# Way down of a seven-product FFN: five groups of four blocks and a tail of two, instead of four groups, a small one and a tail of four

## The chip, the cores and the metric

The kernel runs on one core of a Trainium2 chip. It is one launch, and the metric is the device time of that launch in microseconds (us), taken from several runs of the same program. TensorE (PE in the profile, with PEld for its weight loads) multiplies, VectorE (DVE), ScalarE (ACT) and GpSimd (POOL) work on tiles, SyncE (SP) issues most DMAs and ScalarE some.

## The reference, cut to what matters

One layer of a hybrid decoder on 1024 prompt rows and 32 sample rows, width 1024, hidden width 2816. Four mixers stand between two FFNs; the change touches the FFNs and the norms behind them.

```python
def swiglu(x, wg, wu, wd):
    return (jax.nn.silu(x @ wg) * (x @ wu)) @ wd

def trunk_layer(x, p, gla_h0, rwkv_s0, shift0, pasts):
    ng = p['norms']
    h = x + 0.5 * rms_norm(swiglu(rms_norm(x, ng[0]), p['ff_gate'][0], p['ff_up'][0], p['ff_down'][0]), ng[1])
    cols = rms_norm(h, ng[2]) @ p['w_in']
    ...
    mix = jnp.concatenate([o_gla, o_gmlp, o_rwkv, o_dil], axis=-1) @ p['w_out']
    h = h + rms_norm(mix, ng[3])
    h = h + 0.5 * rms_norm(swiglu(rms_norm(h, ng[4]), p['ff_gate'][1], p['ff_up'][1], p['ff_down'][1]), ng[5])
```

## The kernel before

**Operands.** Everything is float32. Each matrix operand is kept as two parts, hi and lo, in the type that TensorE multiplies fast (`fp32r`); a product is three matmuls, hi·hi, hi·lo and lo·hi. So each operand has to be *split* before use: ACT copies x into hi, and POOL or DVE subtracts, lo = x - hi. Where DVE subtracts, `lower` lets ACT copy x into a PSUM bank first (`via`, tag "pt", two banks).

**Stages of an FFN.** The 2816 hidden columns are 22 blocks of 128. (1) The head makes the first two blocks with ordinary products (`gu`, `act`). (2) `body` makes the other 20 in ten pairs, each pair with one `seven` for gate and one for up, so 20 calls of `seven` per FFN. (3) `way_down` multiplies the blocks, read back from DRAM, with the third weight. (4) `tail` adds the last blocks by ordinary products, row tile after row tile, and runs the norm and the residual (`follow`, `inverse`) on each tile as it becomes ready. In the trace the first FFN's body runs to about 505 us, its way down to 721, its tail to 778, followed by the opening products of the mixers, which wait for the tiles that `follow` has normalised. In the second FFN the body runs from 1833 to 2276, the way down to 2492, and the tail to the end at 2554.

**`seven`** (L549-608) computes four blocks of a product by Winograd's scheme of seven block products; since the prompt rows are taken in three thirds of 352 columns, it has eleven products of 12 matmuls each (`prod`, L540-547). Weights A11, A12, A21, A22 are blocks as they are, S1 to S4 are sums of them. Its operands t1 to t4 are sums of the inputs; `sums` builds them once per FFN, in V (DVE) and G (POOL) operations with splits by `lower`. Results gather in PSUM: Y (tag "pg"), V ("pu"), Z ("pd"), C1 and C2 (both "pt"), two banks a tag. Y gathers S2, S3 and A22 on top of A11; after A11, S2 and S3 an ACT copy (L578) takes the partial sum out before the next product goes on top of it. Order of the products: Y A11, C1 A11, C1 A12, Z A12, C2 A21, Y S2, V S1, Y S3, C2 A22, Y A22, V S4. Only A11, A12, A21 with C1, Z, C2, and A22 with C2, use inputs without sums. `blocks` makes the eight weights in pairs in the order (A11, A12), (A21, S2), (S1, S3), (A22, S4), each in one of four rotating buffers.

**`way_down`** (L778-825) goes through groups of hidden blocks by another seven-product scheme: `GROUPS` has four groups of 4 blocks and one of 2, `NR` = 18, four "rest" blocks for the tail. Each group has four steps (`NS` = 20), a step for a pair of token tiles. A step has seven products of 6 matmuls of 512 columns (3 in the last, small group), all at L712 (`product`). Around each product hang small jobs: `hidden(s + 1)`, in seven parts, forms and splits the next step's hidden operands (POOL sums, ACT copies, DVE subtractions through `via`); `fetch(s + 2)` issues three DMAs that read hidden blocks; `jobs` hands out the next group's weight loads (`raws`), weight forms (`form`, seven per group) and the products of the 32 sample rows (`sample`, L685, 32-column strips). `late` and `split_rest` prepare the tail's operands during the last two groups. What the first group needs is begun by hooks in the last `seven` of the body (`begin_down`, `first_forms`). `Places` and `FORMS` say where each of these lies in SBUF.

**Order.** The engines do not simply follow the file: a list scheduler fixes the order on each engine beforehand, by simulated times and dependencies. In the tails (a loom of generators, `keep(KA)` and `keep(KE)`) DVE and POOL keep the order in which instructions were given.

**Tail norms.** `gain_rows` loads a gain row; for the norms behind the FFNs POOL halves it (L238). `follow` multiplies a tile by the gain on POOL (L287), `inverse` gets the inverse root on DVE from nine or so 128x1 operations (L263 to L273), and L292 multiplies by it and adds the residual.

Of the kernel before, what the change touches and what calls it, by code (L numbers as in the profile page):

```python
# [50 lines left out]
class Layer:  # L51
# [176 lines left out]
    def gain_rows(self, g, half):  # L228

        nc, src = self.nc, self.I["norm_gains"][0]  # L230
        self.junk = self.xs.tile([128, D], mybir.dt.bfloat16, name="junk", tag="s2")
        self.gr = [self.sp.tile([128, n], F32, name="gr", tag=t, bufs=b) for n, t, b in ((D, "n3", 1), (256, "ta", 2))]
        self.dma(self.gr[0], src[g:g + 1].to_broadcast([128, D]))
        for j in range(4):
            self.dma(self.gr[1][32 * j:32 * j + 32], src[g:g + 1, 256 * j:256 * j + 256].to_broadcast([32, 256]))
        if half:
            for x in self.gr:
                nc.gpsimd.tensor_scalar(x, x, 0.5, None, op0=OP.mult)  # L238

    def inverse(self, parts, i):  # L240

# [27 lines left out]
        for _ in range(3):  # L269
# [3 lines left out]
            nc.vector.scalar_tensor_tensor(y, t, 1.5, y, op0=OP.add, op1=OP.mult)  # L273
        yield
        return y

    def follow(self, y, i, name, res, out, hn=None, nxt=None):
# [10 lines left out]

        r = yield from self.inverse([(v[:, cs], (name, i, j), gained(cs)) for j, cs in enumerate(halves)], i)
        rv = res.view(i)  # L290
# [56 lines left out]

GROUPS = [(4 * i, 4) for i in range(4)] + [(16, 2)]
NR = 18
NS = 4 * len(GROUPS)  # L350


class Ffn:
# [86 lines left out]
    def sums(self):  # L440
# [13 lines left out]
        for k in range(KH):  # L454
# [14 lines left out]
            for i, (x, (hi, lo)) in enumerate(((t1, s1[k]), (t2, self.xt[0][k]), (t3, self.xt[1][k]), (t4, self.xt[2][k]))):  # L469
                nc.scalar.copy(hi, x)  # L470
                self.lower(lo, x, hi)
                if i == 1:
                    yield
            yield

    def via(self, x):


        n = x.shape[1:]
        p = self.L.ps.tile([128, 512], F32, name="via", tag="pt", bufs=2)[:, :int(np.prod(n))]  # L480
        if len(n) == 3:
# [3 lines left out]

    def lower(self, lo, x, hi):
        self.L.nc.vector.tensor_tensor(lo, self.via(x), hi.bitcast(F32), op=OP.subtract)  # L487

# [60 lines left out]
    def seven(self, c, j, sil, hooks={}):  # L549
# [26 lines left out]
        def copy(i, p):  # L576
            v = self.temp(i)
            nc.scalar.copy(v, p)  # L578
            return v

        self.prod(Y, A11, self.b11, True)
# [95 lines left out]
    def sample(self, g, which):  # L677
# [3 lines left out]
        strips = [i for i in which if i in (0, 3)], [i for i in which if i in (1, 2)]  # L681
        for j in range(4):
            at = [(i, u) for i in strips[j // 2] for u in range(n)]
            for i, u in at:
                nc.tensor.matmul(p[32 * j:32 * j + 32, :256], self.h8[:, i // 2 * n + u], self.B[i][:, u, j % 2 * 256:j % 2 * 256 + 256],  # L685
                                 start=(i, u) == at[0], stop=(i, u) == at[-1], skip_group_check=True)
        m = 128 if strips[1] else 64
# [3 lines left out]
    def form(self, g, i):  # L691
# [12 lines left out]
        for f in range(n):  # L704
            nc.gpsimd.tensor_tensor(lo[:, f], v[:, f], hi[:, f].bitcast(F32), op=OP.subtract)  # L705
        self.forms[g, i] = hi, lo
# [24 lines left out]
    def split_rest(self, i):  # L731
# [5 lines left out]
        nc.gpsimd.tensor_tensor(lo, x, hi.bitcast(F32), op=OP.subtract)  # L737
        if i < 3:
            self.fetch_rest(i + 1)

    def jobs(self, g, p):
# [3 lines left out]

        last = g + 2 == len(GROUPS)
        if g + 1 == len(GROUPS):
            return self.late(p)
        if p == 0:
            out = [(1, lambda: self.form(0, 4)), (2, lambda: self.sample(0, (3,))), (4, lambda: self.form(0, 6))] if g == 0 else [(1, lambda: self.form(g, 6))]  # L750
            return out + [(5, lambda: self.raws(g + 1, range(4 if last else 3)))]
        if p == 1:
            return [(0, lambda: self.sample(g + 1, range(4 if last else 3)))] + forms((1, 0), (3, 1)) + [(4, lambda: self.fetch_rest(0))] * last
        if p == 2:
            return forms((1, 2), (3, 3)) + [(4, (lambda: self.split_rest(0)) if last else lambda: self.raws(g + 1, (3,)))]
        return [(1, lambda: None if last else self.sample(g + 1, (3,))), *forms((1, 4), (3, 5))] + [(5, lambda: self.split_rest(1))] * last

# [7 lines left out]
    def late(self, p):  # L765

        L = self.L

        def ends():
            self.ends(self.hg[-1], 4)  # L770
# [71 lines left out]

FORMS = ((0, 1, 2, 3, 4, 5, 6), (7, 8, 9, 10, 11, 0, 1), (4, 5, 2, 3, 6, 7, 8), (9, 10, 11, 0, 1, 4, 5))


class Places:
# [28 lines left out]
    def raw(self, g, i, room, n):  # L875
        if g + 1 == len(GROUPS):
            return self.rw[i // 2][:, i % 2 * 512:i % 2 * 512 + 512]
        return (self.r0 if g == 0 else room.rearrange("p a b -> p (a b)"))[:, :1024] if i == 0 else self.rw[min(i - 1, 1)]

    def form(self, g, i):  # L880
        if g + 1 == len(GROUPS):
            v = self.x[2 + i // 2][i % 2] if i < 6 else self.x[5][0]
            return v[:, :512], v[:, 512:1024]
        u = FORMS[g][i]
# [6 lines left out]
    def rest(self, i):  # L891
        return [self.ya[:, k * T:k * T + TP] for k in (2 * (i ^ 2), 2 * (i ^ 2) + 1)]

# [2236 lines left out]
```

## Time and profile before

| | |
|---|---|
| median of 3 runs | 2565.74 us (2552.23 to 2567.77) |
| the profiled execution | 2555.89 us |
| its span in the trace | 2554.2 us |
| mean granted TensorE clock over the span | 0.971 |
| matmuls / VectorE / ScalarE / GpSimd instructions | 15519 / 3249 / 2285 / 948 |

The profile shows one execution: for each engine its busy time and, in the list of waits, what ended its idle time. A row of a timeline is start and duration in us, engine, source line, operation, output <- inputs, shape, and in brackets the idle time ahead of it with what released it. A row of the table by stage is the window, its length, then busy us (and instructions) of PE, PEld, DVE, ACT and POOL, the granted clock as a share of full speed, the share of DMA time and GB/s. A group row has busy us and mean ns of one, then the idle time ahead. Neighbouring matmuls overlap, so a single row shows a latency that is longer than the distance between starts; prices are taken from distances.

### The profile page before, as it was taken

The page shows a single profiled execution, that of the slowest core. Times are in us where ns is not written, and L with a number is a line of the kernel's source. Part 1 is how long each engine was busy: PE and PEld are TensorE (multiplying, and loading weights), DVE is VectorE, ACT ScalarE, POOL GpSimd, SP SyncE. Part 2 cuts the span into 40 slices and gives each one's busy share as a digit, 9 for nine tenths or more (in the row PEclk, how much of TensorE's full clock was granted, in tenths as well). Part 3 has the DMA queues.
Part 4 walks back from the last instruction along what each step waited for, and adds up shares of the span by engine and source line. Part 5 has one row for each costly group of instructions (what it writes and reads, how often), then busy time and mean ns, then how long its engine had stood idle before and what let it go on. Part 6 is the DMA issues. An engine that isn't in the chain of part 4 may idle for free. (4 is left out here: it accounts for less than half of the span.)

```text
span 2554.2 us, 41284 instructions
## 1 busy us (share of the span) xinstructions
PE 2447.9 (96%) x15519; PEld 2226.6 (87%) x15519; DVE 1417.8 (56%) x3249; ACT 1050.2 (41%) x2285; POOL 1093.1 (43%) x948
## 2 busy tenths in 40 slices
PE   8999999999989999999999999998999999999988
PEld 7999999967789988888888888867899999987767
DVE  7545454457776046765532567338834444446767
ACT  5433333466545243233225434335533333356642
POOL 3655555577543232242111111115255555557653
PEclk9999999999999999999989899998999999999998
DMA  4222222333333332331226667254122222233323
GB/s 130 76 72 84 68 84 70 99 103 92 109 125 120 103 105 76 90 103 50 73 68 199 188 189 229 81 185 138 66 63 82 67 83 67 84 103 100 105 88 137
DMA packets 277582, 265.23 MB, mean 104 GB/s; under 512 B 36667, under 2 KB 251860, under 8 KB 277382
## 3 DMA queue, kind: packets, MB, share of 16 engines
q1 hardware_dynamic: 227778, 212.69, 28.2%
q10 hardware_dynamic: 49604, 49.90, 5.7%
q8 instruction: 122, 2.00, 0.3%
q14 instruction: 78, 0.64, 0.1%
HBM read 195.26 MB, written 67.16 MB: 103 GB/s over the span
## 5 line engine op out<-in xcount | busy, mean ns | idle before, releaser
L516 POOL TENSOR_TENSOR wlo<-wraw,whi 128x512 fp32r<-128x512 f32 x280 | 379.4, 1373 | 329.6 <-ACT whi L515 328.9
L545 PE MATMUL p<-xh,whi 128*128 128x352 f32 x1120 | 364.1, 325 | 4.5 <-DVE hid L487 4.5
L547 PE MATMUL p<-xh,wlo 128*128 128x352 f32 x1120 | 362.6, 324 | 0.0
L546 PE MATMUL p<-xl,whi 128*128 128x352 f32 x1120 | 361.6, 323 | 0.0
L515 ACT CAST whi<-wraw 128x512 fp32r<-128x512 f32 x280 | 166.4, 620 | 407.2 <-PE p L546 293.3
L139 PE MATMUL pw<-xh,whi 128*128 128x352 f32 x888 | 309.5, 349 | 2.8 <-ACT stg L2733 2.3
L112 POOL TENSOR_TENSOR wlo<-wraw,whi 128x1024 fp32r<-128x1024 f32 x61 | 145.8, 2392 | 369.3 <-ACT whi L111 327.5
L142 PE MATMUL pw<-xl,whi 128*128 128x352 f32 x888 | 296.4, 334 | 0.0
L143 PE MATMUL pw<-xh,wlo 128*128 128x352 f32 x888 | 294.9, 332 | 0.0
L545 PEld LDWEIGHTS p<-xh,whi 128*128 128x128 f32 x1120 | 211.7, 189 | 4.8 <-DVE hid L487 4.8
L546 PEld LDWEIGHTS p<-xl,whi 128*128 128x128 f32 x1120 | 211.9, 189 | 0.0
L547 PEld LDWEIGHTS p<-xh,wlo 128*128 128x128 f32 x1120 | 210.9, 188 | 0.0
L139 PEld LDWEIGHTS pw<-xh,whi 128*128 128x128 f32 x888 | 172.2, 194 | 12.2 <-issue 6.0
L142 PEld LDWEIGHTS pw<-xl,whi 128*128 128x128 f32 x888 | 172.8, 195 | 2.8 <-issue 1.9
L143 PEld LDWEIGHTS pw<-xh,wlo 128*128 128x128 f32 x888 | 172.3, 194 | 1.9 <-issue 1.2
L545 PE MATMUL p<-hid,whi 128*128 128x352 f32 x400 | 130.0, 325 | 1.2 <-ACT n L578 1.2
L547 PE MATMUL p<-hid,wlo 128*128 128x352 f32 x400 | 130.0, 325 | 0.0
L546 PE MATMUL p<-hid,whi 128*128 128x352 f32 x400 | 129.5, 324 | 0.0
L712 PE MATMUL p<-xh,hid 128*128 128x512 f32 x336 | 113.8, 402 | 5.2 <-DVE hid L788 2.8
L788 DVE TENSOR_TENSOR y<-y,p 128x512 f32<-128x512 f32 x124 | 83.5, 683 | 36.8 <-PE p L712 33.6
L111 ACT CAST whi<-wraw 128x1024 fp32r<-128x1024 f32 x61 | 64.0, 1049 | 92.9 <-PE pw L142 53.2
L788 DVE TENSOR_TENSOR hid<-hid,p 128x512 f32<-128x512 f32 x124 | 83.7, 683 | 32.0 <-PE p L712 28.1
(657 smaller groups left out, 6014.2 us busy)
## 6 DMA issues: line engine op xcount, KB each, us to landing
wraw<-in_w_ff_gate_dram SPq DMA_DIRECT2D x44, 512.0 KB, 3.7
wraw<-in_w_ff_up_dram SPq DMA_DIRECT2D x44, 512.0 KB, 4.0
wraw<-in_w_in_dram SPq DMA_DIRECT2D x37, 512.0 KB, 5.2
wraw<-in_w_ff_down_dram SPq DMA_DIRECT2D x32, 512.0 KB, 3.6
hid_d<-tmp ACTq DMA_DIRECT2D x60, 176.0 KB, 1.9
hid_d<-n ACTq DMA_DIRECT2D x60, 176.0 KB, 2.1
whi<-hid_d SPq DMA_DIRECT2D x72, 128.0 KB, 3.5
cv<-in_cache_win_dram SPq DMA_DIRECT2D x36, 256.0 KB, 3.2
```

The costliest lines, as they stand in the source:

```text
L111: nc.scalar.copy(hi, raw)
L112: nc.gpsimd.tensor_tensor(lo, raw, hi.bitcast(F32), op=OP.subtract)
L139: ins = nc.tensor.matmul(out, a, xh[:, cs], start=(first and i == 0), stop=False)
L142: nc.tensor.matmul(out, a, xl[:, cs], start=False, stop=False)
L143: nc.tensor.matmul(out, b, xh[:, cs], start=False, stop=(last and i == n - 1))
L515: nc.scalar.copy(t[0][:, i], v)
L516: nc.gpsimd.tensor_tensor(t[1][:, i], v, t[0][:, i].bitcast(F32), op=OP.subtract)
L545: nc.tensor.matmul(out, ah, xh, start=first and k == 0, stop=False, skip_group_check=True)
L546: nc.tensor.matmul(out, ah, xl, start=False, stop=False, skip_group_check=True)
L547: nc.tensor.matmul(out, al, xh, start=False, stop=k == KH - 1, skip_group_check=True)
L712: nc.tensor.matmul(out, a[i][:, u], b[j][:, u], start=first and u == i == j == 0, stop=u == n - 1 and i == 1, skip_group_check=True)
L788: (nc.vector.tensor_copy if i % 2 else nc.scalar.copy)(v, p) if copy else nc.vector.tensor_add(v, v, p)
```

## The change

- `GROUPS` becomes five groups of four, `NR` = 20, two rest blocks. `NS` stays 20; the special cases of the small group go from `jobs`, `Places.raw` and `Places.form`; `FORMS` has five rows; `late` fetches, loads and splits the rest during the last group.
- `seven`: the products without sums, C1 and C2, come first, then Z, V S1, and S2, S3 and A22 of Y with their copies, then V S4. The hooks move.
- `sums` puts its `via` copies into "pd" instead of "pt".
- The last `seven` starts group 0 of the way down sooner: `sample` and forms 0 and 1 at hook 5, `fetch(0)` and form 2 at hook 8, the hidden operands and form 3 at hook 9.
- In group 0, forms of odd number split their lo through `via` and DVE instead of on POOL.
- `sample` goes round the strips in turn instead of finishing one after another.
- The gain is not halved on POOL; `inverse` halves its result with one 128x1 DVE operation.

```diff
-        if half:
-            for x in self.gr:
-                nc.gpsimd.tensor_scalar(x, x, 0.5, None, op0=OP.mult)
+        self.half = half
...
         yield
+        if half:
+            nc.vector.tensor_scalar(y, y, 0.5, None, op0=OP.mult)
+            yield
         return y
...
-GROUPS = [(4 * i, 4) for i in range(4)] + [(16, 2)]
-NR = 18
+GROUPS = [(4 * i, 4) for i in range(5)]
+NR = 20
...
-                self.lower(lo, x, hi)
+                self.lower(lo, x, hi, "pd")
...
         done(0, 0, C1, None if j else self.temp(1))
-        hooks.get(3, lambda: None)()
+        hook(3)
+        self.prod(C2, A21, self.lo0, True)
+        self.prod(C2, A22, self.hi0)
+        done(1, 0, C2, None if j else self.temp(4))
+        hook(5)
         self.prod(Z, A12, self.b21, True)
         nc.vector.tensor_add(u, u, Z)
         done(0, 1, u, u)
-        self.prod(C2, A21, self.lo0, True)
+        self.prod(V, S1, self.t1, True)
         self.prod(Y, S2, t2)
         u = copy(7 if j else 2, Y)
-        hooks.get(6, lambda: None)()
-        self.prod(V, S1, self.t1, True)
-        hooks.get(7, lambda: None)()
+        hook(8)
         self.prod(Y, S3, t3)
         w = copy(8 if j else 3, Y)
-        hooks.get(8, lambda: None)()
-        self.prod(C2, A22, self.hi0)
+        hook(9)
         nc.vector.tensor_add(w, w, V)
         done(1, 2, w, w)
-        done(1, 0, C2, None if j else self.temp(4))
         self.prod(Y, A22, t4)
         done(1, 1, Y, None if j else self.temp(5))
         self.prod(V, S4, self.b22)
...
-        for j in range(4):
-            at = [(i, u) for i in strips[j // 2] for u in range(n)]
-            for i, u in at:
...
+        at = [[(i, u) for i in strips[j // 2] for u in range(n)] for j in range(4)]
+        for t in range(2 * n):
+            for j, v in enumerate(at):
+                for i, u in v[t:t + 1]:
...
         for f in range(n):
-            nc.gpsimd.tensor_tensor(lo[:, f], v[:, f], hi[:, f].bitcast(F32), op=OP.subtract)
+            if g == 0 and i % 2:
+                self.lower(lo[:, f], v[:, f], hi[:, f])
+            else:
+                nc.gpsimd.tensor_tensor(lo[:, f], v[:, f], hi[:, f].bitcast(F32), op=OP.subtract)
...
-        return {3: lambda: (self.mem.open(), self.raws(0, range(3))), 6: lambda: self.fetch(0),
-                7: lambda: (self.mem.open_y8(), self.sample(0, range(3)), self.form(0, 0), self.form(0, 1)), 8: self.first_forms}
+        return {3: lambda: (self.mem.open(), self.raws(0, range(3))), 5: lambda: (self.mem.open_y8(), self.sample(0, range(3)), self.form(0, 0), self.form(0, 1)),
+                8: lambda: (self.fetch(0), self.form(0, 2)), 9: self.first_forms}
...
-        for i in (2, 3):
-            self.form(0, i)
+        self.form(0, 3)
         self.raws(0, (3,))
         self.fetch(1)
...
-        return [[(1, lambda: self.form(len(GROUPS) - 1, 6)), (2, ends), (3, lambda: self.wide(0)), (3, lambda: self.wide(1))],
-                [(1, lambda: self.split_rest(2)), (4, lambda: self.wide_parts(0)), (5, lambda: self.wide(2))],
-                [(1, lambda: self.split_rest(3)), (4, lambda: self.wide_parts(1)), (5, lambda: self.wide(3))],
-                [(4, lambda: self.wide_parts(2))]][p]
+        return [[(1, lambda: self.form(len(GROUPS) - 1, 6)), (2, ends), (3, lambda: self.fetch_rest(0)), (6, lambda: self.wide(0))],
+                [(0, lambda: self.wide(1)), (4, lambda: self.split_rest(0))],
+                [(1, lambda: self.wide_parts(0)), (2, lambda: self.wide(2)), (4, lambda: self.split_rest(1))],
+                [(1, lambda: self.wide_parts(1)), (2, lambda: self.wide(3)), (6, lambda: self.wide_parts(2))]][p]
...
-FORMS = ((0, 1, 2, 3, 4, 5, 6), (7, 8, 9, 10, 11, 0, 1), (4, 5, 2, 3, 6, 7, 8), (9, 10, 11, 0, 1, 4, 5))
+FORMS = ((0, 1, 2, 3, 4, 5, 6), (7, 8, 9, 10, 11, 0, 1), (2, 3, 4, 5, 6, 7, 8), (9, 10, 11, 0, 1, 2, 3), (4, 5, 6, 7, 8, 9, 10))
```

More of the change, by code (lines that the diff above doesn't have):

```diff
@@ L235, in gain_rows, with inverse @@
             self.dma(self.gr[1][32 * j:32 * j + 32], src[g:g + 1, 256 * j:256 * j + 256].to_broadcast([32, 256]))
-        if half:
-            for x in self.gr:
-                nc.gpsimd.tensor_scalar(x, x, 0.5, None, op0=OP.mult)
-    def inverse(self, parts, i):
+        self.half = half
+    def inverse(self, parts, i, half=False):
         nc, n = self.nc, len(parts)
@@ L287, in gained @@
             return lambda: nc.gpsimd.tensor_tensor(v[:, cs], v[:, cs], self.gr[i == 8][:, cs], op=OP.mult)
-        r = yield from self.inverse([(v[:, cs], (name, i, j), gained(cs)) for j, cs in enumerate(halves)], i)
+        r = yield from self.inverse([(v[:, cs], (name, i, j), gained(cs)) for j, cs in enumerate(halves)], i, self.half)
         rv = res.view(i)
@@ L474, in sums, with via @@
             yield
-    def via(self, x):
+    def via(self, x, tag="pt"):
         n = x.shape[1:]
-        p = self.L.ps.tile([128, 512], F32, name="via", tag="pt", bufs=2)[:, :int(np.prod(n))]
+        p = self.L.ps.tile([128, 512], F32, name="via", tag=tag, bufs=2)[:, :int(np.prod(n))]
         if len(n) == 3:
@@ L484, in via, with lower @@
         return p
-    def lower(self, lo, x, hi):
-        self.L.nc.vector.tensor_tensor(lo, self.via(x), hi.bitcast(F32), op=OP.subtract)
+    def lower(self, lo, x, hi, tag="pt"):
+        self.L.nc.vector.tensor_tensor(lo, self.via(x, tag), hi.bitcast(F32), op=OP.subtract)
     def begin(self):
@@ L579, in copy, with hook @@
             return v
+        def hook(i):
+            hooks.get(i, lambda: None)()
         self.prod(Y, A11, self.b11, True)
@@ L681, in sample @@
         strips = [i for i in which if i in (0, 3)], [i for i in which if i in (1, 2)]
-        for j in range(4):
-            at = [(i, u) for i in strips[j // 2] for u in range(n)]
-            for i, u in at:
-                nc.tensor.matmul(p[32 * j:32 * j + 32, :256], self.h8[:, i // 2 * n + u], self.B[i][:, u, j % 2 * 256:j % 2 * 256 + 256],
-                                 start=(i, u) == at[0], stop=(i, u) == at[-1], skip_group_check=True)
+        at = [[(i, u) for i in strips[j // 2] for u in range(n)] for j in range(4)]
+        for t in range(2 * n):
+            for j, v in enumerate(at):
+                for i, u in v[t:t + 1]:
+                    nc.tensor.matmul(p[32 * j:32 * j + 32, :256], self.h8[:, i // 2 * n + u], self.B[i][:, u, j % 2 * 256:j % 2 * 256 + 256],
+                                     start=t == 0, stop=t == len(v) - 1, skip_group_check=True)
         m = 128 if strips[1] else 64
@@ L737, in split_rest @@
         nc.gpsimd.tensor_tensor(lo, x, hi.bitcast(F32), op=OP.subtract)
-        if i < 3:
+        if NR + i + 1 < NF:
             self.fetch_rest(i + 1)
@@ L744, in forms @@
             return [(u, lambda i=i: self.form(g + 1, i)) for u, i in x]
-        last = g + 2 == len(GROUPS)
         if g + 1 == len(GROUPS):
@@ L750, in jobs @@
             out = [(1, lambda: self.form(0, 4)), (2, lambda: self.sample(0, (3,))), (4, lambda: self.form(0, 6))] if g == 0 else [(1, lambda: self.form(g, 6))]
-            return out + [(5, lambda: self.raws(g + 1, range(4 if last else 3)))]
+            return out + [(5, lambda: self.raws(g + 1, range(3)))]
         if p == 1:
-            return [(0, lambda: self.sample(g + 1, range(4 if last else 3)))] + forms((1, 0), (3, 1)) + [(4, lambda: self.fetch_rest(0))] * last
+            return [(0, lambda: self.sample(g + 1, range(3)))] + forms((1, 0), (3, 1))
         if p == 2:
-            return forms((1, 2), (3, 3)) + [(4, (lambda: self.split_rest(0)) if last else lambda: self.raws(g + 1, (3,)))]
-        return [(1, lambda: None if last else self.sample(g + 1, (3,))), *forms((1, 4), (3, 5))] + [(5, lambda: self.split_rest(1))] * last
+            return forms((1, 2), (3, 3)) + [(4, lambda: self.raws(g + 1, (3,)))]
+        return [(1, lambda: self.sample(g + 1, (3,))), *forms((1, 4), (3, 5))]
     def wide(self, j):
@@ L765, in late @@
     def late(self, p):
-        L = self.L
         def ends():
-            self.ends(self.hg[-1], 4)
+            self.ends(self.hg[-1], NF - NR)
             self.last = {f: self.h8[:, i] for i, f in enumerate(self.rest)}
-        return [[(1, lambda: self.form(len(GROUPS) - 1, 6)), (2, ends), (3, lambda: self.wide(0)), (3, lambda: self.wide(1))],
-                [(1, lambda: self.split_rest(2)), (4, lambda: self.wide_parts(0)), (5, lambda: self.wide(2))],
-                [(1, lambda: self.split_rest(3)), (4, lambda: self.wide_parts(1)), (5, lambda: self.wide(3))],
-                [(4, lambda: self.wide_parts(2))]][p]
+        return [[(1, lambda: self.form(len(GROUPS) - 1, 6)), (2, ends), (3, lambda: self.fetch_rest(0)), (6, lambda: self.wide(0))],
+                [(0, lambda: self.wide(1)), (4, lambda: self.split_rest(0))],
+                [(1, lambda: self.wide_parts(0)), (2, lambda: self.wide(2)), (4, lambda: self.split_rest(1))],
+                [(1, lambda: self.wide_parts(1)), (2, lambda: self.wide(3)), (6, lambda: self.wide_parts(2))]][p]
     def way_down(self):
@@ L875, in raw @@
     def raw(self, g, i, room, n):
-        if g + 1 == len(GROUPS):
-            return self.rw[i // 2][:, i % 2 * 512:i % 2 * 512 + 512]
         return (self.r0 if g == 0 else room.rearrange("p a b -> p (a b)"))[:, :1024] if i == 0 else self.rw[min(i - 1, 1)]
     def form(self, g, i):
-        if g + 1 == len(GROUPS):
-            v = self.x[2 + i // 2][i % 2] if i < 6 else self.x[5][0]
-            return v[:, :512], v[:, 512:1024]
         u = FORMS[g][i]
@@ L891, in rest @@
     def rest(self, i):
-        return [self.ya[:, k * T:k * T + TP] for k in (2 * (i ^ 2), 2 * (i ^ 2) + 1)]
+        return [self.ya[:, k * T:k * T + TP] for k in (2 * i, 2 * i + 1)]
 class Residual:
```

## The prediction, made before the changed kernel was built or run

> **What bounds the kernel now.** The page comes first: one core, and TensorE is busy for all but a few per cent of the span. Such a kernel gains only where TensorE does less or waits less, so the next view is the list of what TensorE waited for, then the table by stage, then the timelines of the stages that the change touches. The profiled execution took 2555.89 us, of which the span is
>
> ```profile
> span 2554.2 us, 41284 instructions
> ...
> PE 2447.9 (96%) x15519; PEld 2226.6 (87%) x15519; DVE 1417.8 (56%) x3249; ACT 1050.2 (41%) x2285; POOL 1093.1 (43%) x948
> ```
>
> so 1.7 us lie around the span. The median of the three runs, 2565.74, is 9.9 us above it. I sum against the profiled execution and add the result to the median.
>
> TensorE's waits, those of the two FFNs (line, what it waited for, us in total, times, longest):
>
> ```profile
> PE p L712 <- ACT hid L636: 7.5, 2, 4.6
> ...
> PE p L712 <- POOL ya L705: 4.8, 2, 2.6
> PE p L712 <- DVE hid L788: 4.6, 3, 2.8
> PE p L545 <- DVE hid L487: 4.5, 1, 4.5
> ...
> PE p L545 <- ACT sums L470: 4.0, 1, 4.0
> ...
> PE p L545 <- ACT n L578: 3.6, 2, 2.4
> ```
>
> L545 is a product of `seven`, L712 one of the way down. The reader is to see that each wait happens once or twice: they belong to the first `seven`, the start of the way down and its last, small group. By stage (PE, PEld, DVE, ACT, POOL busy, granted clock):
>
> ```profile
> 100.00:470.00 370.00, 370.00 (x2312) 370.00 (x2311) 175.08 (x193) 124.40 (x243) 210.42 (x158) 1.00 0.26 79
> ```
>
> ```profile
> 500.00:540.00 40.00, 35.07 (x156) 24.96 (x155) 21.64 (x37) 26.35 (x46) 23.19 (x22) 0.91 0.33 99
> ```
>
> ```profile
> 2276.00:2306.00 30.00, 25.85 (x109) 16.27 (x107) 14.46 (x25) 19.98 (x33) 21.82 (x23) 0.94 0.41 126
> ```
>
> In the steady `seven`s TensorE is never idle: 370 us for 2312 matmuls, 0.160 us each, 1.92 us for a product of 12. There the change can only lose. At the two starts of the way down it is idle 4.9 and 4.2 us, and loses more at a low clock.
>
> **The change part by part.**
>
> *More products in the way down.* Twenty blocks instead of 18 go through the seven-product scheme: 20 steps of 42 matmuls are 840; before, 16 of 42 and 4 of 21 made 756. The price of one, and of a tail matmul (L204, 256 columns):
>
> ```profile
> 2485.39 0.50 PE L204 MATMUL pt<-whi,ya 128*128 128x256 f32 x2 [0.43 <-ACT whi L111]
> ...
> 2486.55 1.56 PE L712 MATMUL p<-xh,hid 128*128 128x512 f32 x6
> 2487.95 0.40 PE L712 MATMUL p<-xl,hid 128*128 128x512 f32 x1
> ```
>
> ```profile
> 2500.00:2520.00 20.00, 20.00 (x170) 20.00 (x170) 1.00 0.40 139
> ...
> 2485.00:2545.00 60.00, 49.44 (x384) 48.82 (x384) 0.94 0.39 137
> ```
>
> Six way-down matmuls start over 1.40 us, 0.233 each; 170 tail matmuls fill 20 us, 0.118 each. So +84 x 0.233 = +19.6 us per FFN, all on TensorE.
>
> *The small group goes.* Its products (3 matmuls, 0.7 us) are too short to hide the chain that forms the next step's hidden operands; hence the waits on L636 and L788. The stretch from its first to its last product, L712 alone:
>
> ```profile
> 687.90:720.80 32.90, 24.34 (x88) 18.04 (x86) 0.90 0.33 100
> 2457.90:2492.20 34.30, 23.97 (x88) 17.75 (x86) 0.90 0.26 78
> ```
>
> 84 products need 19.6; 30 and 34 early L204 need 3.5 and 4.0. What is left, 9.8 and 10.7 us, is waiting and low clock. A step of 42 gives the chain twice the cover, as in every earlier group, where TensorE is full. I take both as gone (bounds: half to all). What is late next is the split of the two rest blocks, with half the work.
>
> *Sample rows.* The order of the 32-column strips changes, the last group's sample doubles (16 to 32 matmul instructions), and the tail's sample halves:
>
> ```profile
> 569.00:573.00 4.00, 2.83 (x24) 1.41 (x24) 1.00 0.52 156
> ```
>
> ```profile
> 2523.00:2527.00 4.00, 3.62 (x64) 1.98 (x64) 1.00 0.74 263
> ```
>
> The tail's four strips in turn cost 0.057 us an instruction, 24 of `sample` 0.12. Five samples nearer the former save up to 0.8 each, the larger last one costs 1.3: -2 us per FFN in the way down (bounds -3 to +1).
>
> *First operands sooner.* Of group 0, three forms leave GpSimd for a copy by ACT and a subtraction by DVE:
>
> ```profile
> L705 POOL TENSOR_TENSOR ya<-wraw,ya 128x512 fp32r<-128x512 f32 x32 | 41.2, 1304 | 26.8 <-ACT ya L703 26.8
> ...
> L483 ACT COPY via<-wraw 128x512 f32<-128x512 f32 x56 | 32.3, 587 | 19.6 <-DVE wlo L487 15.0 <-DVE hid L487 3.3 <-DVE wraw L702 0.8
> ```
>
> Six times 1.30 us leave POOL, where they stood in front of what TensorE waited for (2.6 us in the first FFN); six times 0.59 come to ACT, which is busy 26 of 40 us there. `fetch(0)` is issued later on SP's queue, behind the first three raw loads; its 3 DMAs stay 3, and its data is old by then. In all SP issues two DMAs fewer (two rest blocks fewer). I take -4 us per FFN (bounds 0 to -9).
>
> *Start of the body.* The first `seven` waits because `via` copies of the sums hold both "pt" banks that C1 and C2 want; with "pd" they hold Z's. Five products without sums, 9.6 us, can run instead of two. Of the waits of 4.5 us in the first FFN and 4.0 in the second, and of the 3.6 us on L578 that the two share, I take 5 in each FFN (bounds 0 to -12, all of them in one). The cover is the weights of A22, now wanted fifth instead of ninth: their buffer is free at the end of the `seven` before, 7.7 us earlier.
>
> *Copies between accumulations.* Y gathers S2, S3 and A22 with a copy out between. Before, another product stood in each gap; now S2, S3, A22 follow one another. The copies on ACT in a steady `seven`:
>
> ```profile
> 302.44 0.62 ACT L515 CAST whi<-wraw 128x512 fp32r<-128x512 f32 x1 [2.29 <-PE p L546]
> 302.97 0.45 ACT L578 COPY n<-p 128x352 f32<-128x352 f32 x1
> ...
> 306.76 0.62 ACT L515 CAST whi<-wraw 128x512 fp32r<-128x512 f32 x1 [2.82 <-DVE wraw L526]
> ```
>
> The copy takes 0.45 and stands behind a cast of 0.53: up to 1.0 us a gap, 80 gaps in 40 `seven`s. I price it at nothing because instructions do not run in the file's order: in the timeline above, tail matmuls (L204) run in front of way-down ones (L712) that come earlier in the file. The A11 products of the next `seven` are independent and have weights since the sixth product. If that cover is missing: 80 x 0.45 = 36 to 80 x 1.0 = 80 us (the rival below).
>
> *Gains' half.* Two POOL multiplications per FFN go; nobody waited for them. Nine DVE instructions come, at the price of a row of that shape:
>
> ```profile
> 2512.01 0.14 DVE L267 TENSOR_SCALAR rq<-rq 128x1 f32<-128x1 f32 x1
> ```
>
> 1.3 us per FFN on DVE, counted in the tail.
>
> *The tail.* 384 matmuls become 192: -22.7 us for TensorE. But the tail also runs the residual and norm of nine row tiles on DVE:
>
> ```profile
> 2505.00:2551.00 46.00, 36.80 (x317) 34.63 (x316) 39.29 (x99) 9.19 (x26) 17.88 (x13) 0.89 0.37 132
> 2493.00:2551.00 58.00, 48.80 (x418) 46.63 (x416) 45.80 (x116) 12.08 (x34) 25.36 (x18) 0.91 0.37 133
> 721.00:812.00 91.00, 81.92 (x622) 77.84 (x621) 75.36 (x265) 55.04 (x143) 35.55 (x23) 0.92 0.41 131
> ```
>
> In the last tail (the second row) DVE is busy 45.8 of 58 us; with 1.3 more, 47.1 is the floor, so at most 11 us can go. I take -5: the time before 2505, the difference of the first two rows: of 12 us TensorE is busy 12.0 and DVE 6.5. In the first FFN the floor is 75.4 + 1.3 of 91, and the opening products behind the tail, which wait for normalised tiles, move up with it: -12 (bounds 0 to -14).
>
> Sum. Way down: 19.6 - 2 - 3.5 - 9.8 - 4 = +0.3 and 19.6 - 2 - 4.0 - 10.7 - 4 = -1.1 (early L204 are counted in the tail). Tails -12 and -5, body starts -5 and -5, copies 0: -28 us. 2555.9 - 28 = 2528 against the profiled execution; 2565.7 - 28 = 2538 against the median.
>
> **Rivals.** *The copies are not covered.* The schedule is fixed beforehand, and the second copy stands behind a cast that waits for DVE (2.82 above); a filler too short leaves TensorE waiting. At 0.85 us a gap it is +68: 2606. It cancels the gain from 0.35 us a gap and makes the kernel over 1% slower from 0.67. Two waits show what else it might cost:
>
> ```profile
> 96.60 0.43 PE L545 MATMUL p<-hid,whi 128*128 128x352 f32 x1 [1.23 <-ACT n L578]
> ```
>
> ```profile
> 514.08 0.80 PE L712 MATMUL p<-ya,whi 128*128 128x512 f32 x1 [2.61 <-POOL ya L705]
> ```
>
> After 1.23 us of waiting for the very copy the next matmul takes 0.43 us from start to end; after 2.61 us it takes 0.80. So I let a gap of up to 1 us cost itself and no clock. The Trainium skill, page "TensorE: Matmul & The Clock Gate", section "What's actually happening", has the clock halve after an idle window of about 3.4 us; by that rule too these gaps cost only themselves, though the row at 514 shows a low clock after less. Against this rival speaks the steady stretch without one idle slot.
>
> *The tails do not gain.* DVE keeps its order in them, and the chain from last matmul to last store stays. The chain of waits between 2480 and 2554, by line:
>
> ```profile
> by line: PE pt L204 25.1%; DVE y L292 12.4%; DVE rq L271 11.0%; PE p L712 10.9%; DVE y L214 10.4%; DVE rq L273 8.4%; DVE rq L263 6.5%; ACT junk L249 3.5%; issue 2.2%; ACT whi L111 1.4%; DVE rq L267 1.3%; DVEq L3126 0.9%; PE pnorm L261 0.8%;
> ```
>
> DVE has half of it. Without the 17 us: 2555, no change. *The starts stay*, since the scheduler orders products itself: 2538 + 10 + 8 = 2556. *All of it comes*: all four starts at their far bounds, another -7 for each body and -5 for each way down, -24 together: 2514.
>
> **How the numbers follow.** Forecast 52%, with 2520 to 2556 as its own range: tails 0 to -25 either way of -17, and the half-kept starts. Copies uncovered 22%, tails without gain 14%, starts without 6%, all of it 6%. One per cent is about what a measurement of this kernel tells from no change: below 2540 is faster, above 2591 slower. Of the forecast's 52, 34 lie below 2540 and 18 above; with the 6 of the best case faster is 40%. Same: 18 + 14 + 6 and 4 of the copies' 22, 42%. Slower: the other 18. The range 2512 to 2590 leaves out those 18 and little below.
>
> **What would show it.** Right: no TensorE wait on L636 near the end of the way down; first `seven` with five products before the first wait; 840 L712 and 192 tail matmuls per FFN, with DVE near full in both tails. Wrong: in the table by stage a steady stretch with idle TensorE and waits of L545 on L578; or a tail of 58 us as before.

## The result and the profile after

The changed kernel takes 2634.39 us (median of 4 runs, 2630.99 to 2636.46) against 2563.53 us before: ratio 1.0282, 95% interval 1.0246 to 1.0319. It is slower by 2.8%, where 2538 was forecast with 2512 to 2590 as the range. The profiled execution, from the page (first lines: the span, then each engine's busy time, share and instructions):

```profile
span 2629.3 us, 40872 instructions
...
PE 2453.3 (93%) x15271; PEld 2204.7 (84%) x15271; DVE 1444.8 (55%) x3289; ACT 1063.3 (40%) x2301; POOL 1075.8 (41%) x942
```

TensorE has 248 instructions less and is busy 5 us more; it waits more. The list of waits of the changed kernel (what waited for what: us in total, times, longest):

```profile
PE p L546 <- ACT tmp L579: 23.5, 20, 1.3
PE p L546 <- ACT n L579: 22.8, 20, 1.2
...
PE p L546 <- ACT whi L516: 3.8, 1, 3.8
...
PE p L546 <- DVE sums L488: 3.2, 1, 3.2
...
PE p L720 <- ACT whi L640: 1.4, 1, 1.4
...
PE p L720 <- ACT hid L640: 0.7, 1, 0.7
```

L546 to L548 are now the lines of `prod`, L579 is the copy of Y, L720 the way down. A new wait stands on top: 40 times, once in every call of `seven`, a product waits for the copy; it is the sign of being wrong that the prediction named. The waits of the way down are nearly gone: 7.5 us on L636, in two waits near its end, became 0.7 and 1.4 on L640, the same line of `hidden`, at the start of the second way down. To see where the span grew, I take five edges from the timeline of TensorE: the first product of the body, the last one of the way down, the first one of the mixers (`prw`), and the same in the second FFN. Before and after, the first three of them:

```profile
71.77 0.32 PE L545 MATMUL p<-xh,whi 128*128 128x352 f32 x1
...
720.44 0.39 PE L712 MATMUL p<-xh,wlo 128*128 128x512 f32 x1
...
846.57 0.23 PE L1064 MATMUL prw<-ident,NT 22*128 22x22 f32 x1
```

```profile
70.50 0.32 PE L546 MATMUL p<-xh,whi 128*128 128x352 f32 x1
...
750.22 0.40 PE L720 MATMUL p<-xh,wlo 128*128 128x512 f32 x1
...
874.83 0.23 PE L1063 MATMUL prw<-ident,NT 22*128 22x22 f32 x1
```

With the other edges (1833.40 and 2491.72 before, 1892.36 and 2578.43 after) the difference of the spans, 75.1 us (the medians differ by 70.9), divides like this:

| stretch | before | after | difference |
|---|---|---|---|
| up to the first `seven` | 71.8 | 70.5 | -1.3 |
| first FFN, body and way down | 648.7 | 679.7 | +31.0 |
| first tail and opening products | 126.1 | 124.6 | -1.5 |
| mixers and the norm behind them, to the second body | 986.8 | 1017.5 | +30.7 |
| second FFN, body and way down | 658.3 | 686.1 | +27.8 |
| last tail | 62.5 | 50.9 | -11.6 |

Three things are to be explained: the FFNs, the mixers, in which no line was changed, and the tails. The steady stretch of the body in the table by stage (window, its length, busy us and instructions of PE, PEld, DVE, ACT, POOL, granted clock, DMA share, GB/s), after:

```profile
100.00:470.00 370.00, 351.23 (x2141) 342.11 (x2140) 163.51 (x177) 113.70 (x229) 194.44 (x147) 1.00 0.23 71
```

2312 matmuls became 2141 in the same 370 us: 22.81 us for a call of 132 instead of 21.12, so 1.69 us lost in each call, 68 us if all 40 lose as much. The two FFN stretches grew by 59, since other parts of them became shorter: the first way down by 3.4 us, the waits at the start of the second body by another 3.4. One call in the timelines of TensorE, ScalarE and VectorE:

```profile
303.30 0.32 PE L548 MATMUL p<-xh,wlo 128*128 128x352 f32 x1
304.83 0.43 PE L546 MATMUL p<-hid,whi 128*128 128x352 f32 x1 [1.21 <-ACT tmp L579]
305.09 0.32 PE L547 MATMUL p<-hid,whi 128*128 128x352 f32 x1
305.25 0.33 PE L548 MATMUL p<-hid,wlo 128*128 128x352 f32 x1
```

```profile
300.36 0.62 ACT L516 CAST whi<-s 128x512 fp32r<-128x512 f32 x1
303.81 0.62 ACT L516 CAST whi<-wraw 128x512 fp32r<-128x512 f32 x1 [2.82 <-DVE wraw L527]
304.33 0.44 ACT L579 COPY tmp<-p 128x352 f32<-128x352 f32 x1
```

```profile
301.95 1.77 DVE L527 TENSOR_TENSOR wraw<-wraw 128x512 f32<-128x512 f32 x1
```

The last matmul of S3 began at 302.32. Six matmuls of the next call's A11 fill the time to 303.46, then TensorE stands until the copy is out at 304.77. ScalarE was idle from 301 on; the copy was late because a cast of the next call's weights stood in front of it and waited for a sum on VectorE. Before, the same cast stood in front of the same copy with the same 2.82 us of waiting, and TensorE lost nothing: there a product of 12 matmuls, 1.92 us, filled the gap. The other six matmuls of that A11 fill the gap behind S2, where some 0.26 us are lost. The view's idle time alone (18.8 us in 370) understates the loss (370 - 2141 x 0.160 = 27.4 us): the second matmul after a gap starts 0.26 us behind the first instead of 0.16, and the last matmul ahead of a gap counts as busy for its whole 0.32.

### The profile page after: what moved, and what is told of

Same layout as the page of the kernel before. It is cut to its first block, busy times and chain, and to the rows that moved or that the text cites. A ratio compares the mean times of both kernels' runs of the same rounds, so it can differ in the third digit from the quotient of the medians.

```text
span 2629.3 us, 40872 instructions
## 1 busy us (share of the span) xinstructions
PE 2453.3 (93%) x15271; PEld 2204.7 (84%) x15271; DVE 1444.8 (55%) x3289; ACT 1063.3 (40%) x2301; POOL 1075.8 (41%) x942
## 4 chain that ended last, share of the span: by engine, by line
PE 66%; DVE 20%; DMA 4%; issue 4%; ACT 3%; POOL 3%; SPq 0%; DVEq 0%; ACTq 0%; POOLq 0%
PE p L720 13%; PE p L546 7%; PE p L548 7%; PE p L547 7%; PE pw L139 5%; PE pw L142 5%; PE pw L143 4%; DVE wraw L522 3%; DVE wraw L527 2%; DVE wraw L531 2%; PE pz L2847 2%; PE pm L2015 1%; POOL wlo L517 1%; DVE rq L269 1%; DVE s L523 1%
## 5 line engine op out<-in xcount | busy, mean ns | idle before, releaser
L546 PE MATMUL p<-xh,whi 128*128 128x352 f32 x1120 | 365.4, 326 | 7.0 <-ACT whi L516 3.8
L548 PE MATMUL p<-xh,wlo 128*128 128x352 f32 x1120 | 363.9, 325 | 0.8 <-POOL wlo L517 0.8
L112 POOL TENSOR_TENSOR wlo<-wraw,whi 128x1024 fp32r<-128x1024 f32 (+1 forms) x61 | 138.0, 2264 | 403.4 <-ACT whi L111 347.3
L546 PEld LDWEIGHTS p<-xh,whi 128*128 128x128 f32 x1120 | 212.1, 189 | 8.4 <-ACT whi L516 4.1
L548 PEld LDWEIGHTS p<-xh,wlo 128*128 128x128 f32 x1120 | 211.5, 189 | 1.3 <-POOL wlo L517 1.3
L546 PE MATMUL p<-hid,whi 128*128 128x352 f32 x400 | 134.7, 337 | 23.0 <-ACT tmp L579 11.6
L548 PE MATMUL p<-hid,wlo 128*128 128x352 f32 x400 | 130.1, 325 | 0.0
L720 PE MATMUL p<-xh,hid 128*128 128x512 f32 x368 | 126.4, 397 | 0.0
L111 ACT CAST whi<-wraw 128x1024 fp32r<-128x1024 f32 (+1 forms) x61 | 60.5, 992 | 112.8 <-PE pw L142 59.5
L546 PEld LDWEIGHTS p<-hid,whi 128*128 128x128 f32 x400 | 75.9, 190 | 34.5 <-ACT tmp L579 17.4
```

Of the source, the lines that this page charges most:

```text
L112: nc.gpsimd.tensor_tensor(lo, raw, hi.bitcast(F32), op=OP.subtract)
L546: nc.tensor.matmul(out, ah, xh, start=first and k == 0, stop=False, skip_group_check=True)
L548: nc.tensor.matmul(out, al, xh, start=False, stop=k == KH - 1, skip_group_check=True)
L720: nc.tensor.matmul(out, a[i][:, u], b[j][:, u], start=first and u == i == j == 0, stop=u == n - 1 and i == 1, skip_group_check=True)
```

## The experiments

In each, the time is given against the kernel before that ran beside it on the same chip. The stretches come from the same edges as above, from each kernel's own trace.

**e1: the old order of products.**

```diff
-        self.prod(C2, A21, self.lo0, True)
-        self.prod(C2, A22, self.hi0)
-        done(1, 0, C2, None if j else self.temp(4))
         hook(5)
...
+        self.prod(C2, A21, self.lo0, True)
         self.prod(Y, S2, t2)
         u = copy(7 if j else 2, Y)
+        self.prod(V, S1, self.t1, True)
         self.prod(Y, S3, t3)
         w = copy(8 if j else 3, Y)
+        self.prod(C2, A22, self.hi0)
```

> The changed kernel with the order of the products in `seven` as it was before (C2's A21 and A22 and V's S1 back between the accumulations of Y), everything else as changed. Theory A (the copies between Y's accumulations are uncovered: 1.7 us lost in each of 40 calls): the steady stretch is full again, 132 matmuls in 21.1 us, both FFN stretches (first `seven` to last way-down product) shorten by 30 to 34 us from 680 and 686, the whole by 62 to 68 to about 2568. Theory B (what the steady stretch loses comes from the weights of A22 being wanted fifth): the same gain here, told apart by the next kernel. Theory C (the loss is something else of the change, such as ScalarE or VectorE work): under 15 us gained. The middle between the FFNs, 1142 us after and 1113 before, stays at 1142 under every one of these, since its order on TensorE is the changed kernel's.

2572.04 us, ratio 1.0056 (1.0033 to 1.0079). The steady stretch is full again (2312 matmuls in 370 us), the FFNs take 650.9 and 657.8, 29 and 28 us less than the changed kernel (30 to 34 were expected), and the mixers 1016.5. So the order of products costs nearly all that the FFNs lost, and the rest of the change is still no gain: the mixers take it.

**e2: the early products kept, the copies covered.** The order is Y A11, C1, C1, C2 A21, C2 A22, Y S2, Z A12, Y S3, V S1, Y A22, V S4.

> The changed kernel with the products without sums still first (C1 and both of C2 behind Y's A11, so A22 is wanted fifth as changed), but Z A12 between Y's S2 and S3 and V S1 between S3 and A22, so that each copy has a product of 12 matmuls, 1.92 us, beside it. Theory A (uncovered copies): steady stretch full, 21.1 us a call, about 2566, and the first `seven` keeps its earlier start. Theory B (weights of A22 too early): the loss stays, above 2620. Middle unchanged at 1142.

2610.72 us, ratio 1.0206 (1.0169 to 1.0243). Neither theory as stated: part of the loss stays. The steady stretch has 2167 matmuls in 370 us, 22.5 us a call, in the first FFN, and 1798 in 300 us, 22.0, in the second, where a call without loss takes 21.35 (1855 matmuls in 300 us, before). The waits of the steady stretch of e2 in the first FFN:

```profile
PE p L546 <- ACT n L579: 8.2, 8, 1.1
PE p L546 <- ACT tmp L579: 5.1, 8, 0.6
PE p L546 <- DVE tmp L605: 3.0, 8, 0.4
```

Again the copy, now with 1.92 us of cover, and behind it VectorE's addition. On ScalarE a cast stands in front, and waits 3.0 us:

```profile
296.48 0.62 ACT L516 CAST whi<-s 128x512 fp32r<-128x512 f32 x1 [3.02 <-DVE s L523]
297.00 0.45 ACT L579 COPY tmp<-p 128x352 f32<-128x352 f32 x1
```

e2 differs from the old order in three more things: A21 is wanted fourth instead of fifth, A22 fifth instead of ninth, and A12, whose buffer the next weights take, is done with Z only at the seventh place instead of the fourth. e5 and e6 go on from there.

**e3: the kernel before, with the new order alone.** The order of the changed kernel in `seven`, hooks at the places that answer to theirs, nothing else.

> The kernel before with nothing but the new order of the products in `seven`. Theory A or B: it loses by itself what the changed kernel lost in the steady stretch, 60 to 70 us, so about 2630. Theory C: within 15 us of before. Its middle has the order of before on TensorE: 1113 us if the order decides, 1142 if the new order of `seven` lengthened it.

2617.94 us, ratio 1.0235 (1.02 to 1.027): 61 us slower by the one edit. FFNs 679.8 and 692.5, the mixers 990.5, 4 us from before. With e1 this shows that the order of products costs 57 to 65 us, and that it does not lengthen the mixers.

**e4: the kernel before, with the gain's half on VectorE alone.**

```diff
-        if half:
-            for x in self.gr:
-                nc.gpsimd.tensor_scalar(x, x, 0.5, None, op0=OP.mult)
+        self.half = half
...
+        if half:
+            nc.vector.tensor_scalar(y, y, 0.5, None, op0=OP.mult)
+            yield
```

> The kernel before with nothing but the gain's half moved from two GpSimd multiplications to a 128x1 VectorE operation a tile in `inverse` (with its step in the tail's weave). Theory M (the middle's +29 us come from where the weave puts the filler products among the mixers, and any shift in the tail moves them): the middle changes from 1113 us by 5 us or more, either way, though no mixer code is touched; FFN stretches stay at 649 and 658, the last tail at 62 to 64. Rival N (the middle grew because of the tail's smaller matmul count or the way down, not the weave): the middle stays at 1113 within 4 us and the whole within 0.3%.

2559.06 us, ratio 0.9993 (0.9976 to 1.0011). The whole stays, as N had it, but the middle goes from 1113.0 to 1121.6, the mixers in it from 986.8 to 999.5 (990.5 in e3, which has the order of before). The FFNs, 644.7 and 654.9, are 4 and 3 us shorter than in the one trace of before, against M's expectation; whether that is the two GpSimd operations that left them or the difference of two traces isn't told apart. One step more in the weave of the first tail goes with mixers longer by 9 to 13 us, in one trace.

**e5: Z back at the fourth place.**

```diff
         hook(3)
+        self.prod(Z, A12, self.b21, True)
+        nc.vector.tensor_add(u, u, Z)
+        done(0, 1, u, u)
         self.prod(C2, A21, self.lo0, True)
         self.prod(C2, A22, self.hi0)
...
-        self.prod(Z, A12, self.b21, True)
-        nc.vector.tensor_add(u, u, Z)
-        done(0, 1, u, u)
```

> The changed kernel with one product moved: Z A12 back to the fourth place, so that the buffer of (A11, A12) is free after the fourth product as before, not after the sixth. S2, S3 and A22 still follow one another with only the next call's A11, six and six matmuls, between; A22 is still wanted fifth. Theory A (uncovered copies alone): the steady stretch stays at about 22.8 us a call in the first FFN (2141 matmuls in 370 us), the whole above 2615. Theory D (the buffers of the weights come free later, so their sums and casts are pressed together and stand on ScalarE and VectorE in front of the copies): 21.1 to 21.6 us a call, 2270 matmuls or more in 370 us, the whole below 2590.

2620.92 us in one run, FFNs 671.4 and 680.5. The steady stretch of e5:

```profile
100.00:470.00 370.00, 357.68 (x2170) 348.81 (x2171) 146.39 (x180) 117.05 (x233) 191.82 (x148) 1.00 0.24 72
```

22.5 us a call, near theory A and far from D: most of the loss stays when the buffer comes free early but the copies have no cover. (In this order A22 is wanted sixth, not fifth as the expectation says.)

**e6: Z fourth, and the copies covered.** Y A11, C1, C1, Z A12, C2 A22, Y S2, C2 A21, Y S3, V S1, Y A22, V S4.

> The changed kernel with Z A12 fourth as before, A22 in C2 fifth as changed, C2's A21 between Y's S2 and S3, V S1 between S3 and A22: every copy covered by 12 matmuls, the first buffer free as early as before, A22 as early as changed. Theories A and D both: the steady stretch is full (2312 matmuls in 370 us), the whole near 2572, that of the old order. Theory B (weights of A22 wanted too early): 22 us a call or more, above 2595.

2572.01 us, ratio 1.0057 (1.0037 to 1.0078), FFNs 647.4 and 654.1, the shortest with five groups so far. The steady stretch of e6, and ScalarE in it:

```profile
100.00:470.00 370.00, 370.00 (x2314) 370.00 (x2313) 167.81 (x193) 125.37 (x243) 205.90 (x158) 1.00 0.26 79
```

```profile
302.21 0.46 ACT L579 COPY n<-p 128x352 f32<-128x352 f32 x1 [2.40 <-PE p L548]
304.01 0.63 ACT L516 CAST whi<-wraw 128x512 fp32r<-128x512 f32 x1 [1.35 <-PE p L547]
304.55 0.61 ACT L516 CAST whi<-s 128x512 fp32r<-128x512 f32 x1
305.06 0.49 ACT L568 ACTIVATE tmp<-tmp 128x352 f32<-128x352 f32 x1
306.05 0.45 ACT L579 COPY n<-p 128x352 f32<-128x352 f32 x1 [0.50 <-PE p L548]
```

Both copies now wait for TensorE's product (L548) and for nothing else, and TensorE never waits. A22 is wanted fifth here too, so in the steady stretch its early place costs nothing (theory B falls). Cover alone isn't enough, and an early end of A12 alone isn't: e5, without cover, loses 1.4 us a call in the first FFN and 1.2 in the second, and 24.0 and 26.4 us of its two FFN stretches, 50 in all, against e6. e2, with cover and a late end of A12, loses 1.4 and 0.7. e2 and e6 differ by an exchange of Z A12 and C2 A21, so e6 also wants A21 three places later than e2; which of the two it is was not tried. That the late buffer presses sums and casts together, in front of the copy, is what the rows of e2 suggest.

**e7: the new order in the first call alone.** `seven` takes the changed order where c == 1 and j == 0, and the old one in the other 19 calls of each FFN.

> The changed kernel with the new order of products in the first call of `seven` of each FFN alone, the order of before in the other 19. Shows what the early products without sums bring by themselves against the changed kernel with the old order throughout (2572 us, FFN stretches 651 and 658). Theory of the prediction: 5 us less in each FFN, 2562. Rival: nothing within 3 us in each, since the scheduler already draws products without sums ahead. Middle unchanged, 1138 to 1144.

2569.57 us, ratio 1.0053 (1.0035 to 1.0071), FFNs 651.3 and 659.3 against 650.9 and 657.8 in e1: no gain, as the rival had it. The changed kernel's first call shows why:

```profile
77.97 0.32 PE L548 MATMUL p<-xh,wlo 128*128 128x352 f32 x1
82.13 0.66 PE L546 MATMUL p<-xh,whi 128*128 128x352 f32 x1 [3.84 <-ACT whi L516]
```

```profile
80.94 1.66 ACT L516 CAST whi<-wraw 128x512 fp32r<-128x512 f32 x3 [1.34 <-DVE wraw L527]
```

The fifth product, with A22, waits 3.84 us for its weights, whose cast stands on ScalarE behind a sum of the weights on VectorE (L527), and VectorE is then busy with the input sums. With 0.81 us more for the lo part and 1.14 for a copy later, the first call waits 5.8 us; before it was 4.47 and 1.23, 5.7 us.

**e8: e1 once more.**

> The kernel of e1 again: changed kernel, old order in `seven`. One more look at its stretches, to know how far they differ between runs of one program. Expected within 4 us of 651, 1138, 658 and 51.

2568.68 us in one run; stretches 649.7, 1138.4, 658.4 and 51.8. Within 1.2 us of e1.

**e9 to e12: other orders of the mixers.** The tail, the opening and the mixers are woven by a planner that keeps modelled clocks of the engines and puts filler products between the mixers' steps. e9, e11 and e12 move only the phase of its modelled TensorE clock, by 1.4, 0.28 and 2.52 us, on top of e6:

```diff
-        k = int(t / TICK)
+        k = int((t + 1.4) / TICK)
...
-        k = int(now / TICK)
+        k = int((now + 1.4) / TICK)
```

e10 takes the gain's half back to GpSimd, on top of e6.

> The kernel of e6 with one number in the planner that weaves filler products among the mixers: the phase of its modelled clock is moved by 1.4 us (added where the weave divides its time by its tick). No instruction is added or removed, only the order of the mixers' products and of the tail's steps changes. Theory M (the length of the mixers follows the order that the weave gives; 987 us with the order of before, 999 in e4, 1016 to 1022 with the changed kernel's): another order, another length, differing from 1018 by over 5 us; FFN stretches stay at 647 and 654, the last tail at 51. Rival N (the mixers are longer because of something that the way down or the smaller tail leaves behind, such as buffers, clock or transfers): 1016 to 1022 again.

> The kernel of e6 with the gain halved on GpSimd as before, so without the additional VectorE step of `inverse` in the weave. Theory M: another order, another length of the mixers, differing from 1018 by over 5 us; the step of 0.14 us a tile itself is worth 1.3 us at most in each tail. Rival N: 1016 to 1022 again.

> As e9, with the phase moved by 0.28 us: the order is that of the changed kernel for the first 938 of some 4610 products of the mixers, then another. Theory M: the mixers' length differs from 1018 by over 5 us, all of it behind that point. Rival N: 1016 to 1022.

> As e9, with the phase moved by 2.52 us. The planner's own estimate for this order is the longest of the three (997 us against 977 and 980; it gives 976 for the order of before and 990 for the changed kernel's). If the planner's estimate tells the true length, this is the slowest of e9, e11 and e12; if the length is not foreseen by it, the three stand in another order.

| kernel | us | ratio (95% interval) | mixers | last tail |
|---|---|---|---|---|
| e9 | 2561.54 | 1.0031 (1.0010 to 1.0052) | 1001.5 | 51.3 |
| e10 | 2548.24 | 0.9963 (0.9945 to 0.9980) | 1000.1 | 48.4 |
| e11 | 2572.95 | 1.0065 (1.0044 to 1.0087) | 1016.1 | 51.2 |
| e12 | 2546.03 | 0.9961 (0.9943 to 0.9980) | 993.8 | 51.6 |

The FFN stretches of all four lie within 1.3 us of e6. The mixers alone, in the table by stage: before, after, e6, e12.

```profile
846.57:1833.40 986.83, 952.55 (x6757) 842.53 (x6757) 531.86 (x1745) 369.57 (x944) 228.99 (x215) 0.96 0.40 122
```

```profile
874.83:1892.36 1017.53, 966.94 (x6757) 851.38 (x6757) 545.20 (x1745) 368.12 (x940) 230.14 (x216) 0.95 0.39 118
```

```profile
843.11:1862.73 1019.62, 969.83 (x6758) 854.08 (x6757) 544.58 (x1745) 368.56 (x940) 230.42 (x216) 0.94 0.39 118
```

```profile
843.25:1837.00 993.75, 951.05 (x6757) 841.32 (x6757) 538.19 (x1745) 368.64 (x944) 227.57 (x215) 0.96 0.40 121
```

The same instructions (6757 on TensorE, 1745 on VectorE, to within one) take 987 to 1020 us. From before to after TensorE is idle 16.3 us longer and busy 14.4 us longer, at a granted clock of 0.95 instead of 0.96. The length goes with the order on TensorE: with that of before, 986.8 and 990.5 (before, e3); with that of the changed kernel, 1015.6 to 1021.6 in six kernels and seven traces of them; with five others, 999.5, 1001.5, 1000.1, 1016.1 and 993.8. The orders on the other engines change with it, and which of them makes a good or a bad one was not tried. e11 missed its bound of 5 us (1016.1 against 1018). The planner's own estimate does not foresee it: e12, which it holds to be the longest, is the shortest of the new ones.

These lengths are from one trace each, and executions of one kernel scatter: the ten of e9 go from 2550 to 2572, and its trace is of the fastest, so its 1001.5 is likely short. By the whole, e10 and e12 are told from e6 (ratios 0.996 against 1.006, their intervals apart), e9 and e11 are not. e12 settles it for M against N: its way down and its instructions are those of e6, only the order differs, and it is some 25 us faster.

e10 and e12 beat the kernel before by 0.4%, and the changed one by more. Their FFNs (647.8 and 654.4, 648.7 and 654.6) are not told from those of the kernel before (648.7 and 658.3, in e4 644.7 and 654.9); their last tail is 11 to 14 us shorter, and their mixers are still 13 and 7 us longer.

## Why the prediction was wrong

*The copies between accumulations.* This is the first step that failed. I priced them at nothing, since the next call's A11 is independent and the order is not the file's. That product did come forward, but it is 12 matmuls for two gaps: six and six, 0.96 us each. The first gap lacks 0.26 us, the second 1.4. The copy's 0.45 us would have fitted into the second gap; the cast in front of it that waits for VectorE did not. I had its row, with 2.82 us of waiting, before me, and the rival names it, but its price counted only the cast's 0.53 us. e6 against the changed kernel gives the term: 32.3 and 32.0 us, 64 in all, 0.80 us a gap; 50 of them are the cover (e5 against e6), the other 14 went with Z's early place (the changed kernel against e5), which the prediction did not weigh. The rival's 0.85 us a gap and +68 were right in place and in the sum; that its point between two bounds came so close is partly luck, since the two gaps are not alike. Its "a gap costs itself and no clock" holds nearly: the granted clock stays 1.00 in the steady stretch, and 0.1 us is lost at each restart.

*What was not in the sum.* The mixers have no term, since no line of them changes; they took 30.7 us. They are ordered by a planner whose input, the first tail, is changed, and their order changed with it. This is the second step that failed, and it is why the rival's 2606 was still too low: 2606 and 31 are 2637.

*Start of the body.* Five products do not run before the first wait: four do (rows of e7). I took the weights of A22 to be there since their buffer is free 7.7 us earlier; in the first call the buffer isn't what they wait for, but ScalarE and VectorE, busy with the input sums. The wait changed its name and kept its size. In the second FFN the waits fell from 7.6 us to 4.2 (3.2 on the sums and 0.97 on a copy), but e7 shows that the new order brings nothing there over e1, whose body is already 3.5 us shorter than before.

*The way down.* The sum was about right, +0.3 and -1.1 forecast. e1 and e6, whose bodies are full, have way downs (last product of the body to last of the way down) of 217.8 and 218.6, and 215.2 and 217.4, against 215.3 and 215.6 before: 0 to 3 us more. Which term the 3 us belong to isn't shown. The small group's waits went (L636 at the end), as did those of the first operands: in the changed kernel's way down of the first FFN, 0.8 us on xl is all that TensorE waits for ScalarE, VectorE and GpSimd together.

*The tails.* -12 and -5 were forecast, -1.5 and -11.6 came; the sum, -17 against -13, hides that each was wrong. The changed kernel's tails, first the 91 us of the first one, then the last:

```profile
750.00:841.00 91.00, 61.23 (x428) 56.85 (x427) 76.41 (x297) 55.54 (x143) 34.63 (x30) 0.79 0.40 127
```

```profile
2578.00:2629.00 51.00, 26.82 (x222) 25.21 (x220) 42.63 (x126) 12.71 (x35) 23.14 (x18) 0.83 0.48 170
```

In the first, TensorE has 21 us less to do than before (61.2 against 81.9) and VectorE the same (76.4 against 75.4), and the stretch is as long: so TensorE did not set it. What I had wrong is that the opening products would move up. They wait for the first normalised tile (`hn`), and that comes later. Before, and then after, with the first product that takes it:

```profile
748.93 1.15 ACT L303 ACTIVATE hn<-hid,rq 128x1024 f32<-128x1024 f32 x1 [1.54 <-DVE rq L273]
```

```profile
796.78 2.21 ACT L304 ACTIVATE hn<-hid,rq 128x1024 f32<-128x1024 f32 x2 [0.26 <-DVE rq L271]
797.99 2.18 PE L312 MATMUL ptx<-ident,hn 128*128 128x128 f32 x8 [20.13 <-ACT hn L304]
```

The first tile is normalised 28.5 us after the last product of the way down before, and 46.6 after; TensorE is through with the tail and stands for 20.1 us. In the ten other traces with two rest blocks it is 44 to 47 us, in e10 too, which has no additional VectorE step, and in the two others with four rest blocks (e3, e4) 28.5 and 30.2. So the smaller tail comes with a later first tile, behind a chain of VectorE's operations, which run there in the order in which they are given; another order was not tried. Nor was my floor a floor: the same 128x1 operation (L271) takes 0.14 us at 775.96 and 2.18 at 788.84, so VectorE's busy time is not a fixed amount of work. In the last tail it is busy for 42.6 us, where I took 47.1 as the least, and 11.6 us went where I counted on 5 and allowed at most 11.

*Gains' half.* I put 1.3 us on it in each tail. Once the last tail has less for TensorE, it is more: e10 without it has a last tail of 48.4 us, against 51.2 to 51.6 in the three kernels beside it and 51.3 in e6, about 2.9 us, for nine operations that take 1.2 (42.70 and 41.51 us busy in e6 and e10); each figure is of one trace. In e4, with the long tail of before, it costs nothing (62.0 against 62.5).

*Clock.* The Trainium skill, page "TensorE: Matmul & The Clock Gate", section "What's actually happening", puts the loss of clock after an idle window of some 3.4 us. Here the waits of 1.2 us left the granted clock at 1.00, and behind the one of 3.84 us at 82.13 it was 0.50 and the matmuls took 0.5 to 0.66 us instead of 0.32. But shorter waits did the same: 2.61 us in the kernel before at 514.08, 3.18 us in the changed one at 1905.42, and 2.38 us in the second body of the kernel before, of which this is the row, with the table by stage behind it:

```profile
1861.86 0.66 PE L545 MATMUL p<-sums,whi 128*128 128x352 f32 x1 [2.38 <-ACT n L578]
```

```profile
1861.90:1863.40 1.50, 1.50 (x5) 1.50 (x6) 0.46 (x1) 1.28 (x3) 1.50 (x2) 0.50 0.00 0
```

A wait of 2.42 us at 2466.76 left it at 1.00. So here the page's figure and the rows differ, and the rows decide: a wait of some 2.4 us can already halve the clock in these kernels. My allowance, that a gap of up to 1 us costs no clock, stands.

## What to carry to other kernels

An operation between two products can cost what its queue makes it wait, and not only its own duration: before a copy is called covered, look at what stands in front of it on its engine and what that waits for, and count the filler matmuls against the moment at which the copy is out. A product moved forward also moves the moment at which its operands must be there and buffers come free; both can decide whether the order holds in the steady stretch. Where a planner orders a stage, an edit ahead of it can change that stage too, by 30 us of 1000 here with the same instructions: measure stages one by one, and do not credit or blame an edit for the total before the shuffle is told apart.

## What the runs showed of the hardware

A gap of TensorE cost more here than the idle time that the profile shows. In the steady stretch of the changed kernel 18.8 us are shown idle and 27.4 us of matmul starts are missing, in some 16 calls: about half a microsecond a call comes on top, from two restarts (second start 0.26 instead of 0.16 us behind the first) and from last matmuls that count as busy until they end.
